# Head of a hybrid decoder layer: first weight unit in fp32, two chunks by turns, x blocks in pairs

## The chip, the cores and the metric

The kernel runs on one core of a Trainium2 chip. The metric is the device time of one execution in microseconds (us). The five engines of the core have in-order instruction queues of their own: PE multiplies matrices (PEld is its weight load), DVE and ACT do element-wise work, POOL fills memory here, and SP issues nearly all transfers (DMAs).

## The reference

One layer of a decoder trunk, for a sequence of 256 rows and a width of 1024, in fp32:

```
proj = x @ w_in                 # 1024 -> 5120, split into q k v z_a u z_s g_a g_s
y_a  = (attention(q, k, v) * silu(z_a)) @ w_attn_proj
y_s  = s5_ssm(u, ...)           # a state space scan over the rows
y_s  = glu(gelu(y_s) @ w_glu)
y_s  = (y_s * silu(z_s)) @ w_ssm_proj
mix  = (sigmoid(g_a) * y_a + sigmoid(g_s) * y_s) @ w_out
ple  = sigmoid(x @ w_ple_gate) * (p @ w_ple_proj)
out  = layer_norm(alpha * x + mix + ple)
```

What matters here is the first product, `x @ w_in`, and of it the columns of u (512) and of z_a (512). The kernel calls z_a `za`. All products have to keep nearly fp32 precision.

## The kernel before, in words

**Products by split operands.** To multiply in a fast reduced-precision type, fp32r, each operand is split: ACT rounds it to fp32r (the high half: `xh`, `whi`), and DVE subtracts that from the original (the low half: `xl`, `wlo`). A product is then three passes: high by high, low x by high weight, high x by low weight. A few small products, such as those with the tile `Kbd`, are taken in plain fp32.

**Weight units and steps.** The weights are cut into units of 256 rows by 512 columns (512 KB, in the tile `raw`, with 5 buffers). `load_next` issues the load of the next unit on SP, and `split_next` splits it on ACT (line 144) and DVE (line 145) into `whi` and `wlo` (3 buffers each). Each unit has one step on PE: two blocks of 128 rows (k), for each three passes, and for each pass four column blocks, so 24 matmuls (line 149 is the helper that issues every matmul). Four steps make a chunk of 512 columns of `w_in`. The order of the chunks is u, za, zs, q, k, v and so on. In the first chunks (`t_chunk`) x is the moving operand, 256 columns wide, and the weight is the stationary one. A chunk adds up in two PSUM banks of the kind `acc` (4 in all; 4 more, `aux`, are for other work), and when its last step is done, an evacuation (`ev_u`, `ev_za`, ...) brings it to SBUF.

**The head.** Sixteen warm-up matmuls on constants come first (line 87). x is loaded transposed in 8 blocks of 128 KB into `xs` (the tag `sc`). For c = 0 to 3 the code loads, for each of the two k, one block of x and one half of weight unit c, by turns (lines 189 and 191; the very first half in two pieces), and splits the x block (lines 192 and 193). Units 0 and 1 are split in the head in pieces. That is 18 loads; the parameters `par` (line 197) come among them, and unit 4 follows.

**The loop.** For each step i it loads the next unit, evacuates the chunk that ended, and splits a unit that is two steps ahead; then it issues the matmuls of step i, and then other work that is put to a step by number (`at(i, ...)`): parameter loads and scalar work of the state space part after step 0, `s5_bounce` (u is written to DRAM and read back in another order by eight loads, line 449) after step 4, and so on. PE runs in the order of the code. The order on the other engines, SP's queue among them, is laid out by a planner that simulates the schedule at build time, with priorities; head and loop duties have a high one.

Of the kernel before, what the change touches and what calls it, by code (L numbers as in the profile page):

```python
# [10 lines left out]
F32 = mybir.dt.float32  # L11
# [3 lines left out]
AF = mybir.ActivationFunctionType  # L15
# [3 lines left out]
P = 128  # L19
# [38 lines left out]
def hybrid_layer_kernel(ctx: ExitStack, tc, xT, x, pT, w_in, w_ap, w_sp, w_out, par, bp, cp,  # L58
                        dsk, w_glu, w_pg, w_pp, lng, lnb, relb, cst, out):
    nc = tc.nc  # L60
    V, A, G, PE = nc.vector, nc.scalar, nc.gpsimd, nc.tensor
# [5 lines left out]
    def T(shape, tag, dt=F32, bufs=1, nm=None):  # L67
        cnt[0] += 1
        return pool.tile(list(shape), dt, name=f"{nm or tag}_{cnt[0]}", tag=tag, bufs=bufs)

    def PS(tag, bufs):
        cnt[0] += 1
        return ps.tile([P, 512], F32, name=f"{tag}_{cnt[0]}", tag=tag, bufs=bufs)

    def acc():
        return PS("acc", 4)
# [19 lines left out]
    NRAW, NHI, NLO = 5, 3, 3  # L96
    units = []

    def add_units(w, k, c0, n):
        v = w.rearrange("(k p) n -> p k n", p=P)  # L100
        for k0 in range(0, k // P, 2):
            units.append(v[:, k0:k0 + 2, c0:c0 + n])
# [3 lines left out]
    raw, hi, lo = {}, {}, {}  # L106
    st = dict(load=0, split=0)

    def load_next(pieces=1):
        i = st["load"]  # L110
        if i >= len(units):
            return
        st["load"] += 1
        t = T([P, 2, 512], "raw", bufs=NRAW)
        for k in range(pieces):
            w = 2 // pieces
            nc.sync.dma_start(t[:, k * w:k * w + w], units[i][:, k * w:k * w + w])
        raw[i] = t
# [3 lines left out]
    def split_next(pieces=1):  # L122
        i = st["split"]
        if i >= len(units):
            return
        st["split"] += 1
        r = raw.pop(i)
        j = i - (len(units) - 4)
        if j < 0:
            h = T([P, 2, 512], "whi", F32R, NHI)  # L130
            l = T([P, 2, 512], "wlo", F32R, NLO)
        else:
            if j == 0:
                tail_w.update(h0=T([P, 2, 2, 512], "xh", F32R), h1=T([P, 2, 2, 512], "xl", F32R),
                              l0=T([P, 2, 2, 512], "tb", F32R), l1=T([P, 2, 2, 512], "sc", F32R))
            h, l = tail_w[f"h{j // 2}"][:, j % 2], tail_w[f"l{j // 2}"][:, j % 2]
        if pieces == 1:
            cuts = [(slice(0, 2), slice(0, 512))]
        else:
            cuts = [(slice(0, 1), slice(0, 512)), (slice(1, 2), slice(0, 512))]  # L140
            if i == 0:
                cuts[0:1] = [(slice(0, 1), slice(0, 256)), (slice(0, 1), slice(256, 512))]
        for k, c in cuts:
            A.activation(h[:, k, c], r[:, k, c], AF.Copy)  # L144
            V.tensor_sub(l[:, k, c], r[:, k, c], h[:, k, c].bitcast(F32))  # L145
        hi[i], lo[i] = h, l

    def mm(o, a, b, start, stop):
        return PE.matmul(o, a, b, start=start, stop=stop, skip_group_check=True)  # L149


    add_units(w_in, D, COL["u"], 512)
    add_units(w_in, D, COL["za"], 512)
    add_units(w_in, D, COL["zs"], 512)
    add_units(w_in, D, COL["q"], 512)
    add_units(w_in, D, COL["k"], 512)
# [23 lines left out]
    xh = T([P, KD, S], "xh", F32R)  # L180
    xl = T([P, KD, S], "xl", F32R)
    xs = T([P, KD, S], "sc")
    pr = T([P, 3, GP], "par")
    for c in range(4):
        t = T([P, 2, 512], "raw", bufs=NRAW)
        raw[c] = t
        for k in range(2):
            kk = 2 * c + k
            nc.sync.dma_start(xs[:, kk], xT[:, kk])  # L189
            for cc in ((slice(0, 256), slice(256, 512)) if kk == 0 else (slice(0, 512),)):  # L190
                nc.sync.dma_start(t[:, k, cc], units[c][:, k, cc])  # L191
            A.activation(xh[:, kk], xs[:, kk], AF.Copy)  # L192
            V.tensor_sub(xl[:, kk], xs[:, kk], xh[:, kk].bitcast(F32))  # L193
        if c < 2:
            split_next(2)
        if c == 1:
            nc.sync.dma_start(pr, par)
    st["load"] = 4
    load_next()
    br = T([P, 2, GP, 16], "brw")  # L200
    cr = T([P, 2, GP, 16], "crw")

# [160 lines left out]
    def s5_bt(part):  # L363
        b = st5["b"]
        o = st5[f"Bt{part}"] = T([P, 8, 2, 4, 16], f"A{part}")
        t = T([P, 2, 8, 4, 16], f"B{part}")
        for r in range(2):
            g = slice(8 * r, 8 * r + 8)
            ar = bc(st5["Ar"][:, g, 0:4], 3, 16)
            ai = bc(st5["Ai"][:, g, 0:4], 3, 16)  # L370
            b0, b1 = bc(b[:, part, g], 2, 4), bc(b[:, 1 - part, g], 2, 4)
            V.tensor_mul(o[:, :, r], b0, ar)
            V.tensor_mul(t[:, r], b1, ai)
            (V.tensor_add if part else V.tensor_sub)(o[:, :, r], o[:, :, r], t[:, r])
# [247 lines left out]

    steps = []

    def t_chunk(nk, xop, evac):
        st_ = {}

        def step(i, k0, first, last):
            def f(u):
                if first:  # L630
                    st_["a"] = [acc(), acc()]
                xh_, xl_ = xop()
                for k in range(2):
                    kk = k0 + k
                    for a_, b_, z in ((hi[u], xh_, 0), (hi[u], xl_, 1), (lo[u], xh_, 2)):
                        for m in range(4):
                            o = st_["a"][m // 2][:, 256 * (m % 2):256 * (m % 2) + 256]
                            mm(o, a_[:, k, m * P:(m + 1) * P], b_[:, kk, :],
                               first and k == 0 and z == 0 and m % 2 == 0,
                               last and k == 1 and z == 2)  # L640
            return f
        for i in range(nk // 2):
            steps.append([step(i, 2 * i, i == 0, i == nk // 2 - 1), None])
        steps[-1][1] = lambda: evac(st_["a"])
# [24 lines left out]
    xop = lambda: (xh, xl)  # L669
# [59 lines left out]
    def new(key, tag, shape=(P, 2, 512), dt=F32):  # L729
# [3 lines left out]
        return f  # L733

    t_chunk(8, xop, ev_u)
    t_chunk(8, xop, ev_za)
    t_chunk(8, xop, ev_zs)
    t_chunk(8, xop, ev_q)
    t_chunk(8, xop, ev_k)
# [89 lines left out]
    def at(i, *f):  # L829
        order.setdefault(i, []).extend(f)  # L830
# [8 lines left out]
    at(0, *[hp_(f) for f in (s5_scalars, s5_angles, s5_phases)])  # L839
    at(1, hp_(s5_abar))  # L840
    at(2, lambda: s5_bt(0), lambda: s5_bt(1))
    at(4, s5_bounce)
    at(8, a_bias)
    at(5, lambda: s5_ca(0), lambda: s5_ca(1))
    at(6, small_loads)
# [22 lines left out]
    for i, (f, ev) in enumerate(steps):  # L868
        with tc.high_priority():
            load_next()  # L870
            if pend is not None:
                pend()
                pend = None
            split_next(2 if i < 2 else 1)
        f(i)
        for fn in order.pop(i, []):
            fn()
        pend = ev
# [62 lines left out]
    u = nmain  # L941
# [70 lines left out]
```

## Time and profile before

| | before |
|---|---|
| median of 3 runs | 241.86 us (241.4 to 242.76) |
| the profiled execution, its own time | 242.09 us |
| its span, first to last instruction | 240.3 us |
| PE busy | 230.3 us (96%) |
| DVE busy | 188.2 us (78%) |
| ACT busy | 140.2 us (58%) |
| read from HBM | 42.47 MB, 183 GB/s over the span |

The span is what the trace covers; 1.8 us of the execution's time lie around it. Times in the rows below count from the start of the span. A matmul's duration includes the way through the array, so several overlap, and the pace is read from their starts.

### The profile page before, as it was taken

To read this page: it belongs to the slowest core of one execution; us is meant where nothing else is said; L and a number is where in the kernel's file an instruction comes from. 1 tells how busy PE (TensorE), PEld (TensorE's weight loads), DVE (VectorE), ACT (ScalarE), POOL (GpSimd) and SP (SyncE) were. 2 spreads that over 40 slices of the span, in tenths; PEclk is the share of its full clock that TensorE was granted. 3 is DMA by queue.
4 is the path that set the end of the run, shared out by engine and by line. 5 is a ranking of instruction groups with operands and counts; after the bars stand their busy time and mean duration, and the time that the engine had idled before them with its cause. 6 is when DMAs were issued, how large, how long until landed. Compare 5 with 4: busy or idle time off the path is not lost.

```text
span 240.3 us, 5066 instructions
## 1 busy us (share of the span) xinstructions
PE 230.3 (96%) x2042; PEld 212.6 (88%) x2042; DVE 188.2 (78%) x333; ACT 140.2 (58%) x222; POOL 15.9 (7%) x17
## 2 busy tenths in 40 slices
PE   8899999999999999999999999999999999999970
PEld 6899999999978899998998999999888889988760
DVE  2879999999899986878999744485674479997395
ACT  4847554845588389999734955335565353775021
POOL 4000000000000005000000000072000000000031
PEclk9999999999999999999999999999999999999998
DMA  5999998977634484323743663664555655660013
GB/s 162 331 343 357 354 238 242 353 232 215 196 93 118 147 255 119 110 92 97 232 150 136 207 213 110 197 245 162 189 174 191 199 202 170 186 190 0 3 44 131
DMA packets 26374, 44.37 MB, mean 185 GB/s; under 512 B 4200, under 2 KB 7280, under 8 KB 26352
## 3 DMA queue, kind: packets, MB, share of 16 engines
q1 hardware_dynamic: 26064, 43.75, 57.5%
q8 instruction: 16, 0.26, 0.4%
q10 hardware_dynamic: 288, 0.31, 0.4%
q14 instruction: 6, 0.05, 0.1%
HBM read 42.47 MB, written 1.59 MB: 183 GB/s over the span
## 4 chain that ended last, share of the span: by engine, by line
PE 77%; ACT 10%; DMA 5%; DVE 4%; SPq 2%; issue 1%; ACTq 0%
PE acc L149 68%; PE aux L149 8%; DMA raw<-in_w_in 5%; ACT whi L144 4%; ACT sc L587 2%; ACT sc L592 2%; ACT CAb L436 1%; DVE wlo L145 1%; SPq L191 1%; SPq L189 1%; DVE xb L930 1%; DVE xb L920 1%; DVE st L910 1%; DVE xb L908 1%; PE aux L598 0%
## 5 line engine op out<-in xcount | busy, mean ns | idle before, releaser
L144 ACT ACTIVATE whi<-raw 128x1024 fp32r<-128x1024 f32 (+2 forms) x71 | 70.7, 997 | 59.9 <-PE acc L149 52.9
L145 DVE TENSOR_TENSOR wlo<-raw,whi 128x1024 fp32r<-128x1024 f32 (+2 forms) x71 | 81.9, 1154 | 30.3 <-ACT whi L144 29.9
L149 PE MATMUL acc<-xh,whi 128*128 128x256 f32 x288 | 47.7, 287 | 0.8 <-ACT whi L144 0.8
L149 PE MATMUL acc<-xl,whi 128*128 128x256 f32 x288 | 45.8, 281 | 0.0
L149 PE MATMUL acc<-xh,wlo 128*128 128x256 f32 x288 | 45.6, 280 | 0.0
L149 PEld LDWEIGHTS acc<-xh,whi 128*128 128x128 f32 x288 | 39.3, 190 | 2.3 <-ACT whi L144 1.3
L149 PEld LDWEIGHTS acc<-xl,whi 128*128 128x128 f32 x288 | 39.3, 189 | 0.0
L149 PEld LDWEIGHTS acc<-xh,wlo 128*128 128x128 f32 x288 | 38.9, 188 | 0.3 <-DVE wlo L145 0.3
L149 PE MATMUL acc<-whi,xh 128*128 128x512 f32 x48 | 19.0, 395 | 0.0
L149 PE MATMUL acc<-wlo,xh 128*128 128x512 f32 x48 | 19.0, 395 | 0.0
L149 PE MATMUL acc<-whi,xl 128*128 128x512 f32 x48 | 19.0, 395 | 0.0
L149 PEld LDWEIGHTS acc<-wlo,xh 128*128 128x128 f32 x48 | 9.0, 188 | 2.2
L149 PEld LDWEIGHTS acc<-whi,xh 128*128 128x128 f32 x48 | 9.0, 188 | 2.1
L149 PEld LDWEIGHTS acc<-whi,xl 128*128 128x128 f32 x48 | 9.0, 188 | 2.1
L149 PE MATMUL acc<-whi,BT 128*128 128x512 f32 (+1 forms) x32 | 9.1, 366 | 0.0
L818 POOL TENSOR_SCALAR xb<-xb 128x1024 f32<-128x1024 f32 x2 | 5.5, 2774 | 42.2 <-DMA xb<-in_x 42.2
L916 ACT ACTIVATE rs<-mv,eps 128x1 f32<-128x1 f32 x2 | 0.6, 294 | 12.1 <-DVE mv L915 12.1
L587 ACT ACTIVATE sc<-sc,nmx 128x128 f32<-128x128 f32 (+1 forms) x16 | 7.0, 442 | 0.0
L149 PEld LDWEIGHTS acc<-whi,BT 128*128 128x128 f32 x32 | 5.7, 188 | 1.1
L193 DVE TENSOR_TENSOR xl<-sc,xh 128x256 fp32r<-128x256 f32 x8 | 3.4, 420 | 4.1 <-ACT xh L192 4.1
L908 DVE TENSOR_TENSOR xb<-acc,xb 128x512 f32<-128x512 f32 (+1 forms) x4 | 2.5, 619 | 5.0 <-PE acc L149 5.0
L928 POOL TENSOR_TENSOR xb<-xb,lng 128x512 f32<-128x512 f32 (+1 forms) x2 | 1.7, 839 | 69.8 <-ACT xb L927 69.8
(254 smaller groups left out, 407.8 us busy)
## 6 DMA issues: line engine op xcount, KB each, us to landing
raw<-in_w_in SPq DMA_DIRECT2D x36, 512.0 KB, 4.7
raw<-in_w_pg SPq DMA_DIRECT2D x8, 512.0 KB, 4.6
raw<-in_w_out SPq DMA_DIRECT2D x8, 512.0 KB, 4.5
raw<-in_w_ap SPq DMA_DIRECT2D x4, 512.0 KB, 5.0
raw<-in_w_glu SPq DMA_DIRECT2D x4, 512.0 KB, 3.9
raw<-in_w_sp SPq DMA_DIRECT2D x4, 512.0 KB, 4.1
raw<-in_w_in SPq DMA_DIRECT2D x7, 256.0 KB, 4.3
sc<-in_xT SPq DMA_DIRECT2D x8, 128.0 KB, 4.0
```

The costliest lines, as they stand in the source:

```text
L144: A.activation(h[:, k, c], r[:, k, c], AF.Copy)
L145: V.tensor_sub(l[:, k, c], r[:, k, c], h[:, k, c].bitcast(F32))
L149: return PE.matmul(o, a, b, start=start, stop=stop, skip_group_check=True)
L189: nc.sync.dma_start(xs[:, kk], xT[:, kk])
L191: nc.sync.dma_start(t[:, k, cc], units[c][:, k, cc])
L193: V.tensor_sub(xl[:, kk], xs[:, kk], xh[:, kk].bitcast(F32))
L436: A.activation(o[rw, :, :, 16 * g2:16 * g2 + 16], st5[f"CA{part}"][rw, :, 1:5, :], AF.Copy)
L587: A.activation(sc[:, h, qs[q]], sc[:, h, qs[q]], AF.Exp, bias=nmx[:, h, q:q + 1], accum_out=sm_[:, h, q:q + 1])
L592: A.activation(sc[:, h, qs[q]], sc[:, h, qs[q]], AF.Copy, scale=sm_[:, h, q:q + 1])
L818: G.tensor_scalar(late["xb"][:, s, :], late["xb"][:, s, :], ALPHA, None, op0=ALU.mult)
L908: V.tensor_tensor(out=xb[:, s, sl], in0=(yo2 if c0 else yo[s][n])[:, 0:c1 - c0], in1=xb[:, s, sl], op=ALU.add)
L910: V.bn_stats(out=stat[s][:, c // 256, :], in_=xb[:, s, c:c + 256])
```

## The change

The first weight unit is no longer split: it stays in fp32 in `w0`, and step 0 multiplies it by the unsplit x, `xs`, in one fp32 product in place of three passes. The units and the steps of the chunks u and za are put by turns (u, za, u, za, ...), so that two steps in a row read the same two blocks of x; za adds up in `aux` banks. x blocks 2 to 7 are loaded in pairs, and units 1, 2 and 3 as one transfer each. The x splits of blocks 4 to 7 are done in steps 2 and 4. `s5_bounce` comes after step 8.

```
@@ units @@
 add_units(w_in, D, COL["u"], 512)
 add_units(w_in, D, COL["za"], 512)
+units[:] = [units[i + 4 * c] for i in range(4) for c in range(2)]
@@ head @@
-for c in range(4):
-    t = T([P, 2, 512], "raw", bufs=NRAW)
-    raw[c] = t
-    for k in range(2):
-        kk = 2 * c + k
-        nc.sync.dma_start(xs[:, kk], xT[:, kk])
-        for cc in ((slice(0, 256), slice(256, 512)) if kk == 0 else (slice(0, 512),)):
-            nc.sync.dma_start(t[:, k, cc], units[c][:, k, cc])
-        A.activation(xh[:, kk], xs[:, kk], AF.Copy)
-        V.tensor_sub(xl[:, kk], xs[:, kk], xh[:, kk].bitcast(F32))
-    if c < 2:
-        split_next(2)
-    if c == 1:
-        nc.sync.dma_start(pr, par)
-st["load"] = 4
+def load_xT(k0, n=1):
+    nc.sync.dma_start(xs[:, k0:k0 + n], xT[:, k0:k0 + n])
+def split_x(k):
+    A.activation(xh[:, k], xs[:, k], AF.Copy)
+    V.tensor_sub(xl[:, k], xs[:, k], xh[:, k].bitcast(F32))
+w0 = T([P, 2, 512], "raw", bufs=NRAW)
+for k in range(2):
+    load_xT(k)
+    nc.sync.dma_start(w0[:, k], units[0][:, k])
+st.update(load=1, split=1)
 load_next()
+load_xT(2, 2)
+nc.sync.dma_start(pr, par)
+load_next()
+load_next()
+load_xT(4, 2)
+load_next()
+load_xT(6, 2)
+for k in (0, 1):
+    split_x(k)
+split_next(2)
+for k in (2, 3):
+    split_x(k)
@@ t_chunk @@
-def t_chunk(nk, xop, evac):
+def t_chunk(nk, xop, evac, bank=acc):
-                    st_["a"] = [acc(), acc()]
+                    st_["a"] = [bank(), bank()]
-                for a_, b_, z in ((hi[u], xh_, 0), (hi[u], xl_, 1), (lo[u], xh_, 2)):
+                for a_, b_, z in (((hi[u], xh_, 0), (hi[u], xl_, 1), (lo[u], xh_, 2)) if u
+                                  else ((w0, xs, 0),)):
@@ chunks and order @@
-t_chunk(8, xop, ev_za)
+t_chunk(8, xop, ev_za, aux)
+steps[:] = [steps[i + 4 * c] for i in range(4) for c in range(2)]
-at(4, s5_bounce)
+at(8, s5_bounce)
@@ loop @@
-        split_next(2 if i < 2 else 1)
+        if i in (2, 4):
+            for k in (i + 2, i + 3):
+                split_x(k)
+        split_next()
```

## Rows read from the trace of the kernel before

**Rows 1.** The page: busy time, share of the span and instructions.

```profile
PE 230.3 (96%) x2042; PEld 212.6 (88%) x2042; DVE 188.2 (78%) x333; ACT 140.2 (58%) x222; POOL 15.9 (7%) x17
```

**Rows 2.** Chain of waits in order of time: start, us, what.

```profile
9.83 6.41 DMA raw<-in_w_in
...
18.72 13.46 PE acc L149 x112
```

**Rows 3.** Waits, 18.72 to 228 us: us in total, times, longest.

```profile
ACT whi L144 <- PE acc L149: 52.9, 35, 3.2
```

**Rows 4.** Timeline of PE in the head: start, us, instructions, idle before.

```profile
7.39 0.74 PE L149 MATMUL acc<-xh,whi 128*128 128x256 f32 x4 [0.81 <-ACT whi L144]
...
8.91 0.63 PE L149 MATMUL acc<-xh,whi 128*128 128x256 f32 x4
...
11.73 0.63 PE L149 MATMUL acc<-xh,whi 128*128 128x256 f32 x4
...
17.46 0.74 PE L149 MATMUL acc<-xh,whi 128*128 128x256 f32 x4
...
18.72 0.74 PE L149 MATMUL acc<-xh,wlo 128*128 128x256 f32 x4
```

**Rows 5.** Timeline of PE, narrow windows at a plain fp32 product.

```profile
135.46 0.59 PE L149 MATMUL aux<-uT,Kbd 128*128 128x256 f32 x2
...
135.67 0.70 PE L149 MATMUL aux<-uT,Kbd 128*128 128x256 f32 x3
...
135.89 0.71 PE L149 MATMUL aux<-uT,Kbd 128*128 128x192 f32 x4
```

**Rows 6.** Timeline of PE, narrow windows in step 0.

```profile
5.17 0.81 PE L149 MATMUL acc<-xl,whi 128*128 128x256 f32 x3
...
5.38 0.72 PE L149 MATMUL acc<-xl,whi 128*128 128x256 f32 x3
...
5.94 0.63 PE L149 MATMUL acc<-xh,wlo 128*128 128x256 f32 x4
```

**Rows 7.** Timeline of SP: its twelfth and thirteenth load, and unit 6.

```profile
5.88 0.43 SPq L191 DMA_DIRECT2D raw<-in_w_in  x1
...
6.70 0.33 SPq L189 DMA_DIRECT2D sc<-in_xT  x1
...
10.87 0.41 SPq L117 DMA_DIRECT2D raw<-in_w_in  x1
```

**Rows 8.** Timeline of ACT and DVE in the head: splits, idle before.

```profile
5.88 0.42 ACT L192 ACTIVATE xh<-sc 128x256 fp32r<-128x256 f32 x1 [1.35 <-DMA sc<-in_xT]
...
6.70 0.63 ACT L144 ACTIVATE whi<-raw 128x512 fp32r<-128x512 f32 x1 [0.41 <-DMA raw<-in_w_in]
...
16.35 1.06 ACT L144 ACTIVATE whi<-raw 128x1024 fp32r<-128x1024 f32 x1 [2.02 <-DMA raw<-in_w_in]
...
17.44 1.22 DVE L145 TENSOR_TENSOR wlo<-raw,whi 128x1024 fp32r<-128x1024 f32 x1 [1.29 <-ACT whi L144]
```

**Rows 9.** Windows: busy of PE, PEld, DVE, ACT, POOL, clock, DMA share, GB/s.

```profile
0.00:4.00 4.00, 3.24 (x16) 2.27 (x16) 0.46 (x5) 1.96 (x3) 2.88 (x6) 1.00 0.42 121
4.00:6.70 2.70, 2.57 (x14) 2.27 (x12) 1.33 (x4) 0.88 (x3) 0.00 (x0) 1.00 0.81 238
6.70:10.14 3.44, 2.75 (x23) 2.75 (x24) 2.73 (x9) 2.81 (x7) 0.00 (x0) 1.00 1.04 350
10.14:16.25 6.11, 6.11 (x54) 6.11 (x54) 5.61 (x23) 3.36 (x7) 0.00 (x0) 1.00 0.95 323
16.25:20.30 4.05, 4.00 (x33) 3.67 (x32) 2.56 (x5) 3.21 (x6) 0.00 (x0) 1.00 1.05 396
```

**Rows 10.** DMA issues of units 4 and 6: KB each, us to landing.

```profile
raw<-in_w_in SPq DMA_DIRECT2D x1, 512.0 KB, 6.4
...
raw<-in_w_in SPq DMA_DIRECT2D x1, 512.0 KB, 9.4
```

**Rows 11.** Instructions at tile U: durations in ns, first and last start.

```profile
L149 PE MATMUL aux<-U,BT x128: 217/218/267, 93.2 to 105.8; 64*64 64x64 f32 x128
```

## The prediction

> **What bounds the kernel now.** I read the page first: the tensor engine is counted busy for 230.3 of 240.3 us [rows 1]. Such a share alone says little, so the chain of waits in order of time comes next [rows 2]. Before 18.72 its longest piece is a weight load of 6.41 us, and the split of that load ends last. At 18.72 a run of 112 matmuls begins, and the chain stays on PE for most of what follows. The waits after 18.72 agree: ACT waits 52.9 us, in 35 places, for matmuls to free weight buffers before it splits the next unit [rows 3]. So everything from 18.72 on follows the tensor engine's own pace, and the changed stage is worth what it moves that start.
>
> The timeline gives the pace. A step (one weight unit, 24 matmuls of 256 columns) takes 11.73 - 8.91 = 2.82 us, 0.1175 us for each matmul [rows 4]. In the head, step 0 stops half way and goes on at 7.39, after 0.81 us of idle time. Step 1 starts at 8.91. Step 4 starts at 17.46, but its ninth matmul, the first that needs the low half, starts only at 18.72; at the pace it would come 8 x 0.1175 = 0.94 us after the first [rows 4]. So the stream of before is worth an unbroken start of step 4 at 18.72 - 0.94 = **17.78**. The task is to find that moment after the change. It has two clocks: the matmuls and the loads.
>
> **Part 1: unit 0 without a split.** Removed: three ACT pieces, three DVE pieces and 24 matmuls. Added: 8 products in full fp32. The trace has the same kind, the Kbd products of the scan's output: each stands there as two instructions, which for 256 columns start 0.215 us apart (135.67 after 135.46, then 135.89) [rows 5]. Eight products are 16 instructions, 16 x 0.215 = 3.44 us against 2.82 us, so the edit costs PE 0.62 us. From below, two passes at the 0.1175 us of a split matmul would be 1.88 us; I take the row, which has the same tile and the same number of columns. The Trainium skill (FP8 and Floating Point Precision, TensorE Precision Notes) says true fp32 takes four passes through the array. Four passes of 0.1175 us for eight products would be 3.76 us, 0.32 us more than the row gives; the two instructions of the trace, each at nearly double time, agree in kind, and the row decides.
>
> The granted clock reads 1.00 throughout [rows 9], but early matmuls start 0.21 us apart (5.17, then 5.38) and from 5.94 on at the pace of the later steps [rows 6]: 1.2 GHz first, 2.4 GHz from about 5.81, after the engine had worked without a break from 0.8 us on. The first four matmuls therefore began at 5.17 - 4 x 0.215 = 4.31, right behind the warm-up matmuls, and an earlier operand can't move that. Fp32 instructions at the low clock should need 0.43 us (double the row): (5.81 - 4.31) / 0.43 = 3.5 of the first block's eight; the other 4.5 take 0.97 us, so the block ends at 6.78. The second block needs the second x block and weight piece, and takes 8 x 0.215 = 1.72 us: step 0 ends at **8.50**. That is 0.41 us before the 8.91 of before, although the sum of its work grew, since no split stands between load and matmul. Steps 2, 3 and 4 could then start at 11.32, 14.14 and 16.96 (2.82 apart), if their operands are there: 17.78 - 16.96 = 0.82 us gained at most.
>
> **Part 2: the order and size of the loads.** With the chunks by turns, steps 0 and 1 read the same two x blocks, so x blocks 2 and 3 are needed one step later. On SP the head has 12 issues where it had 19. SP shows a limit: its twelfth and thirteenth loads start at 5.88 and 6.70, the moments when the fourth (an x block) and the fifth (a weight piece) have landed, as ACT's waits there show [rows 7, 8]. Eight transfers are in flight at a time; larger ones put more bytes in flight. After the change the ninth to twelfth wait for the first to fourth, so all of 3.7 MB can be issued by about 6.2.
>
> Now bytes. By the windows 484 kB had moved at 4.0 us (4 x 121), 1127 kB at 6.7, and the rate is 350 GB/s from there to 10.14 [rows 9]. The fifth load landed at 6.70 and it and all before it are 786 kB, so a load lands when 341 kB more than its own end have moved. That lag grows with the bytes in flight: the load issued at 9.83 landed 6.4 us later, at 16.25, when 4305 kB had moved and 3694 were needed (611); the one issued at 10.87 landed 9.4 us later, at 20.3, with 5909 moved for 4742 (1167) [rows 7, 9, 10]. For after I take 484 kB at 4.0, 300 GB/s to 6.7 (between the 238 of before, when SP had less in flight, and 350), and 350 from there: 1294 kB at 6.7.
>
> The ends in the new order: second weight piece 786, unit 1 1311, x blocks 2 and 3 1573, parameters 1598, unit 2 2122, unit 3 2646, x 4 and 5 2908, unit 4 3432, x 6 and 7 3695, unit 5 4219 kB. The second weight piece lands at 6.14 (lag 341), before 6.78: no gap in step 0. Unit 1 lands at 6.7 + (1652 - 1294) / 350 = 7.72; its first half is split on ACT in 0.63 us [rows 8], ready at 8.40, just ahead of 8.50. Unit 2 is the tight one: it is now split whole, 1.06 us on ACT and then 1.22 us on DVE [rows 8], so its low half is ready 2.33 us after landing with the hand-overs, and step 2 wants it at 11.32 + 0.94 = 12.26: the landing must not be after **9.93**. With a lag of 341 to 611 it lands between 10.04 and 10.81; I take 10.4. Step 2 then stands still for about 0.45 us. Unit 3 lands at 12.3 with a lag of 611 and has until 14.14 + 0.45 + 0.94 - 2.33 = 13.2; unit 4 (14.6) has until 16.0. Unit 5 is new in one point: its buffer is freed by the last fp32 matmul at 8.50, not by a split, and nothing of the head stands behind it on SP. It needs 4830 kB and lands at 16.8 (18.4 with a lag of 1167), wanted by 19.78 + 0.45 + 0.94 - 2.33 = 18.84.
>
> **Part 3: what is only moved.** The x splits of blocks 4 to 7 (0.42 us a block on ACT [rows 8], and as much on DVE if its time for the same tile is like ACT's) move into steps 2 and 4, two steps ahead of their use, where ACT waits for PE; without that cover each pair would cost about 1.7 us. The u evacuation and the nine transfers of the bounce move four steps, about 11 us, later; the first matmul that reads their result starts at 93.2 [rows 11], so this is hidden, and the parameter loads keep their place behind step 0. The za chunk takes two aux banks instead of acc banks at a time when one aux bank at most is wanted elsewhere. These come to nothing.
>
> **Sum.** 0.82 gained less 0.45 for unit 2: 0.37 us. The profiled execution took 242.09 us with a span of 240.3, so its counterpart is a span of 239.9 and 241.7 us; the median shown is 241.86, which gives 241.5.
>
> **The rivals.** (a) The loads are ample: SP's larger transfers run at 350 GB/s from 4.0 on with a lag of 341, unit 2 lands at 9.65, no stall: 241.0. For it speaks that 350 is reached where the queue is full; against it the slow stretch 4.0 to 6.7. (b) Ample loads, and step 0 shorter too: with the higher clock by 5.0 it ends at 8.07, and the gain is 1.25: 240.6. Nothing in the rows moves the clock forward; cheaper fp32 instructions would do the same, against [rows 5]. (c) The other side: more bytes in flight hold the early ones back. With the lag of 1167 kB already at unit 2, it lands at 6.7 + (3289 - 1294) / 350 = 12.4, step 2 waits 2.5 us, and the kernel is 1.65 us slower: 243.5. It decides from a landing of 10.75 (no gain) and counts as slower from 11.96. Against it: lags that large came only after several transfers of 512 KB. (d) The fp32 passes keep the low clock: 16 x 0.43 from 4.31 ends at 11.19, step 4 starts at 19.65, 1.87 us later: 243.7. The rows show fp32 products only inside a stream already at the higher clock; against it, PE has no gap before them. (e) The change does nothing because the planner orders ACT and DVE anew and a later step pays back the gain: about 241.9.
>
> **How the numbers follow.** Forecast 0.43, with its own range 241.1 to 241.9; (a) 0.16; (b) 0.16; (c) 0.12; (d) 0.06; (e) 0.07. 0.5% is 1.21 us, about what a measurement here can tell from no change; faster ends at 240.65 and slower begins at 243.07. (b) is faster with 0.16 and a little of (a) and of the lower end of the forecast adds 0.02: 0.18. (c) and (d) are slower: 0.18. The rest, 0.64, is the same. The range 240.5 to 243.1 leaves out (c) and (d) and little else.
>
> **What would show it.** Right: two fp32 instructions per product 0.215 us apart, step 0 ending near 8.5, a single short stop before the low half of unit 2, then an unbroken stream to beyond 70 us, about 0.4 us ahead. Wrong: a stop between the two blocks of step 0, unit 2 landing after 10.75, 0.43 us spacing beyond 6 us, or a wait of PE after 25 us that was not there.

## The result

The changed kernel takes 243.53 us in the median (242.49 to 244.07) where the kernel before takes 241.86, seven executions of each: the ratio is 1.0061, 95% interval 1.0034 to 1.0087. Measured once more, beside the last experiments, it was 243.85 us and 1.0070 (1.0051 to 1.0089). The prediction was 241.5 us, a gain too small to count as a change; the change makes the kernel 1.7 us slower. Two executions of it have a trace: 244.01 us with a span of 242.2, and 243.32 us with a span of 241.5. Ratios leave out executions more than 1.5% above the fastest of their kernel; here these are two of the first try at theory L, the one with its trace among them.

The page's shares say nothing of it, as they answer to [rows 1] within 1.5%:

```profile
PE 230.8 (95%) x2034; PEld 211.7 (87%) x2034; DVE 186.8 (77%) x328; ACT 138.3 (57%) x217; POOL 15.9 (7%) x17
```

Where the time went is read from two places in the chain of waits (start, us, what). The kernels before and after both have there, unbroken, a run of 312 matmuls that takes 42.49 us, and far behind it one of 372 matmuls that takes 61.37 us. They cut a span into a head, a middle and a tail. First the chain of the kernel before, further on than [rows 2]:

```profile
32.70 42.49 PE acc L149 x312
...
156.78 61.37 PE acc L149 x372
```

Then that of the changed kernel, with its head:

```profile
4.02 7.79 DMA raw<-in_w_in
11.81 0.02 issue
11.83 1.07 ACT whi L144
12.90 0.02 issue
12.92 1.24 DVE wlo L145
14.16 0.04 issue
14.20 2.15 PE acc L149 x16
...
33.84 42.49 PE acc L149 x312
...
158.76 61.37 PE acc L149 x372
```

The head ends at 33.84 us in place of 32.70. The middle, from one run to the other, takes 158.76 - 33.84 = 124.92 us in place of 124.08. The tail (242.2 - 158.76 = 83.4, 240.3 - 156.78 = 83.5) is the same. So of the 1.9 us between these two traces the head has 1.14 and the middle 0.84. The second trace of the changed kernel has its run of 312 at 32.95 and a middle of 125.09; a second kernel with the head of before (the experiment with p late, below) has 32.88 and 123.92. In the means the head costs 0.6 us (33.40 against 32.79) and the middle 1.0 (125.0 against 124.0): 1.6 of the 1.7 us.

**The head after**, the timeline of TensorE (TensorE, ScalarE and VectorE are the engines that the rows call PE, ACT and DVE). The rows answer to [rows 4]:

```profile
4.59 0.67 PE L149 MATMUL acc<-sc,raw 128*128 128x256 f32 x2 [0.32 <-DMA raw<-in_w_in]
...
4.88 0.59 PE L149 MATMUL acc<-sc,raw 128*128 128x256 f32 x2
...
5.09 0.60 PE L149 MATMUL acc<-sc,raw 128*128 128x256 f32 x2
...
6.93 0.67 PE L149 MATMUL acc<-sc,raw 128*128 128x256 f32 x2 [0.38 <-DMA raw<-in_w_in]
...
9.14 0.74 PE L149 MATMUL aux<-xh,whi 128*128 128x256 f32 x4 [0.24 <-ACT whi L144]
```

Each fp32 product is indeed two instructions, 0.21 us apart. Step 0 ends near 6.93 + 8 x 0.215 = 8.65 (8.50 was forecast). Step 1 starts only at 9.14, since it waits for the split of unit 1, which ScalarE begins at 8.46 (a landing at 7.72 was forecast). Then the chain above: unit 2, issued at 4.02, lands at 11.81, its splits follow at once, and the first matmul that needs its low half starts at 14.20. From there on the engine does not stop before the middle. The loss of the head in this trace follows from this one landing: without it step 4 could have started at 9.14 + 3 x 2.82 = 17.60, still 0.18 us ahead of the 17.78 of before. How much had moved by then is in the windows (busy time of PE, PEld, DVE, ACT and POOL, granted clock, DMA share, GB/s), which answer to [rows 9]:

```profile
0.00:4.00 4.00, 3.24 (x16) 2.25 (x16) 0.23 (x4) 1.57 (x2) 2.88 (x6) 1.00 0.44 122
4.00:6.90 2.90, 2.23 (x10) 1.44 (x8) 0.85 (x2) 0.55 (x2) 0.00 (x0) 1.00 0.89 301
6.90:8.44 1.54, 1.51 (x7) 1.39 (x8) 0.00 (x0) 0.00 (x0) 0.00 (x0) 1.00 0.90 271
8.44:10.00 1.56, 1.32 (x10) 0.91 (x9) 0.69 (x1) 1.15 (x2) 0.00 (x0) 1.00 0.98 358
10.00:11.81 1.81, 1.81 (x17) 1.81 (x17) 1.28 (x7) 0.72 (x2) 0.00 (x0) 1.00 1.06 409
```

Time by rate, 488 + 873 + 417 + 558 + 740, is 3076 kB at 11.81. The forecast's own curve gives 1294 + 350 x 5.11 = 3082 there, so the rate was right. But unit 2 and all before it are 2122 kB: it landed with 954 kB of later loads already moved.

**The middle after.** TensorE's timeline has one long stop, and ScalarE's shows what came late. The longest stop of TensorE in this stretch of the trace of before is 0.47 us, at 80.28; near this one it has 0.23 us, at 112.77.

```profile
111.83 0.72 PE L149 MATMUL acc<-xh,whi 128*128 128x256 f32 x4 [1.04 <-ACT whi L144]
```

```profile
85.82 1.07 ACT L396 ACTIVATE BT<-aux 128x512 f32<-128x512 f32 x2
88.11 0.63 ACT L227 ACTIVATE ph<-Ct 128x512 fp32r<-128x512 f32 x1 [1.23 <-DMA Ct<-in_pT]
88.76 1.28 ACT L598 ACT_TABLE_LOAD   x1
90.06 0.40 ACT L598 ACTIVATE sc<-sc,nmx 128x128 f32<-128x128 f32 x1
...
110.73 2.94 ACT L144 ACTIVATE whi<-raw 128x1024 fp32r<-128x1024 f32 x3
```

The split of p (`ph`) stands in ScalarE's queue ahead of the table load and the exponentials of the softmax, and waits 1.23 us for p's transfer. From 88.11 to the split at 110.73 that TensorE waits for, ScalarE has no idle time, so the wait is passed on in full. The load itself is late because p is put into the tile `Ct`, which the state space part uses too: it is issued at 84.16, when VectorE's last reading of that tile (82.9 plus 1.22 us) has ended (the rows of the tile, and SP's timeline). In the trace of before the two moments lie as close, 85.47 behind 84.2 plus 1.22.

```profile
L417 DVE TENSOR_TENSOR C<-C,Ct x1: 1218/1218/1218, 82.9 to 82.9; 128x1024 f32<-128x1024 f32 x1
```

```profile
84.16 0.66 SPq L226 DMA_DIRECT2D Ct<-in_pT  x1
```

In the kernel before, the planner had put the same split behind the first exponentials:

```profile
84.86 1.06 ACT L385 ACTIVATE BT<-aux 128x512 f32<-128x512 f32 x2
85.94 1.28 ACT L587 ACT_TABLE_LOAD   x1
...
89.81 0.63 ACT L216 ACTIVATE ph<-Ct 128x512 fp32r<-128x512 f32 x1 [0.72 <-DMA Ct<-in_pT]
```

So there are two theories to test. L, for the head: more bytes in flight behind unit 2 hold it back. Q, for the middle: p ahead of the softmax is what the later stop pays for.

### The profile page after: what moved, and what is told of

It reads as the page before. It is cut to its first block, busy times and chain, and to the rows that moved or that the text cites. A ratio compares the mean times of both kernels' runs of the same rounds, so it can differ in the third digit from the quotient of the medians.

```text
span 242.2 us, 5025 instructions
## 1 busy us (share of the span) xinstructions
PE 230.8 (95%) x2034; PEld 211.7 (87%) x2034; DVE 186.8 (77%) x328; ACT 138.3 (57%) x217; POOL 15.9 (7%) x17
## 4 chain that ended last, share of the span: by engine, by line
PE 77%; ACT 10%; DVE 5%; DMA 5%; SPq 1%; issue 1%; ACTq 0%
PE acc L149 66%; PE aux L149 10%; DMA raw<-in_w_in 3%; ACT sc L598 3%; ACT whi L144 2%; ACT CAb L447 2%; ACT sc L603 2%; DMA Ct<-in_pT 2%; DVE wlo L145 1%; DVE xb L946 1%; DVE xb L936 1%; DVE st L926 1%; DVE xb L924 1%; ACT L598 1%; SPq L186 1%
## 5 line engine op out<-in xcount | busy, mean ns | idle before, releaser
L145 DVE TENSOR_TENSOR wlo<-raw,whi 128x1024 fp32r<-128x1024 f32 (+1 forms) x66 | 80.2, 1216 | 32.0 <-ACT whi L144 32.0
L144 ACT ACTIVATE whi<-raw 128x1024 fp32r<-128x1024 f32 (+1 forms) x66 | 68.6, 1045 | 63.1 <-PE acc L149 50.7
L149 PE MATMUL acc<-xh,whi 128*128 128x256 f32 x248 | 40.6, 285 | 1.7 <-ACT whi L144 1.7
L149 PE MATMUL acc<-xh,wlo 128*128 128x256 f32 x248 | 39.4, 280 | 0.1
L149 PE MATMUL acc<-xl,whi 128*128 128x256 f32 x248 | 39.2, 280 | 0.0
L149 PEld LDWEIGHTS acc<-xh,whi 128*128 128x128 f32 x248 | 33.4, 188 | 3.1 <-ACT whi L144 2.2
L149 PEld LDWEIGHTS acc<-xh,wlo 128*128 128x128 f32 x248 | 33.5, 188 | 0.5 <-DVE wlo L145 0.5
L149 PEld LDWEIGHTS acc<-xl,whi 128*128 128x128 f32 x248 | 33.5, 188 | 0.0
L603 ACT ACTIVATE sc<-sc,sms 128x128 f32<-128x128 f32 (+1 forms) x16 | 6.1, 442 | 0.0
```

What stands on the lines that cost most here:

```text
L603: A.activation(sc[:, h, qs[q]], sc[:, h, qs[q]], AF.Copy, scale=sm_[:, h, q:q + 1])
```

## The experiments

In the tables of times "run of 312" is the start of that run in the profiled execution, or of the run of 288 that begins at the same step; "middle" is from there to the run of 372. Ratios are to the kernel before, beside which each was measured.

**One part at a time.** Unit 0 in fp32 alone, in the head of the kernel before:

```
+if c == 0:
+    raw0.append(raw.pop(0)); st["split"] = 1      # unit 0 isn't split
...
+                    else ((raw0[0], xs, 0),)):      # step 0: one product
```

> The kernel before with only unit 0 taken in fp32 without a split; order and size of the loads stay. If the price of the fp32 passes is what costs (16 x 0.215 = 3.44 us against 2.82): 242.5. If step 0 hides it, because its halves wait for loads anyway and no split stands between: step 1 starts at 8.5 to 8.9 and the time is 241.5 to 241.9.

The two chunks by turns alone (units and steps by turns, za in `aux`, `s5_bounce` after step 8):

> The kernel before with only the chunks u and za by turns, za in aux banks, and the bounce after step 8; loads keep their sizes and units 0 and 1 their splits. Theory L: the head is as before or up to 0.3 us earlier, since nothing more is in flight: 241.6 to 241.9. Theory P (the order of work itself, through the planner, costs the later 0.8 us at 104 to 113 us): 242.7, with ACT's split in front of step 31 queued behind normalisations of the attention.

The loads alone (x blocks 2 to 7 in pairs, units 1 to 3 whole, unit 0 in two parts; three passes, chunks one after the other):

```
+nc.sync.dma_start(xs[:, kk:kk + 2], xT[:, kk:kk + 2])
+nc.sync.dma_start(t, units[c])
```

> The kernel before with only the sizes of the head's loads changed: x blocks 2 to 7 in pairs, units 1 to 3 as one transfer each, unit 0 as two; steps and splits in the old order. Theory L: unit 1 lands near 8.9 (it needs 1573 kB, with a lag of some 500), steps 1 and 2 stop, the head is 0.8 to 1.5 us later: 242.7 to 243.4. Rival B: unit 1 lands as its second half did, at 9.0, but its first half was ready 1.1 us sooner before, so 0.5 us at most: 242.4.

| | median us | ratio, interval | run of 312 | middle |
|---|---|---|---|---|
| fp32 alone | 245.48 | 1.0132 (1.0109 to 1.0155) | 32.22 | 129.22 |
| turns alone | 241.87 | 0.9987 (0.9971 to 1.0002) | 32.17 | 124.46 |
| loads alone | 246.76 | 1.0176 (1.0150 to 1.0202) | 32.96 | 127.96 |

None of the three alone costs the head more than 0.2 us against the mean of 32.79, and in these traces two of the parts cost the middle 4 to 5 us that the whole change does not (in the medians 3.3 and 4.6 us, against 242.20 beside them; the trace of fp32 alone is of its longest execution, 246.75). The waits of TensorE behind 60 us (engine, line, waited for: us in total, times, longest) say where, here for fp32 alone:

```profile
PE aux L149 <- ACT ks L720: 2.4, 1, 2.4
PE aux L387 <- DVE nmx L581: 1.3, 1, 1.3
PE aux L387 <- ACT BT L389: 1.1, 1, 1.1
```

All of it is work between 77 and 89 us (`ks` and `nmx` are tiles of the attention, `BT` one of the state space part) whose instructions no edit touched. Behind the stops its granted clock reads 0.66 from 90 to 95 us, so a part of the loss is the lower of its two levels. In the two kernels that lose, VectorE and ScalarE have another order there, though the code of that stretch is the same; with the turns alone it is nearly that of before.

**Theory L, first try: units 1 to 4 in two loads of 256 KB each, x blocks singly.**

```
-load_next(); load_xT(2, 2)
+load_next(2); load_xT(2); load_xT(3)
...
```

> The changed kernel with the same order of loads, but units 1 to 4 in two transfers of 256 KB each and x blocks one by one, so that the limit of eight transfers holds fewer bytes in flight. Theory L (bytes in flight: a load lands late when many bytes behind it are already issued; unit 2 landed at 11.8 us with 3076 kB moved where 2122 were needed): unit 2 lands by 10.8, the stop before step 2 shrinks from 0.68 + 0.25 us to 0.3 or less, the head is about 1.0 us earlier, 242.5 us if the later loss of 0.8 us stays, 241.7 if it goes. Rival B (only order and rate count): unit 2 lands at 11.8 again, 243.5.

Measured: 248.63 to 255.25 us, ratio 1.0321 (1.0270 to 1.0372). The trace is of an execution of 254.98 us; whether the shorter ones stop as long is not shown. ScalarE's timeline shows both halves of the answer:

```profile
10.35 1.06 ACT L144 ACTIVATE whi<-raw 128x1024 fp32r<-128x1024 f32 x1 [0.96 <-DMA raw<-in_w_in]
...
19.77 2.00 ACT L144 ACTIVATE whi<-raw 128x1024 fp32r<-128x1024 f32 x2 [5.96 <-DMA raw<-in_w_in]
```

Unit 2 is there at 10.33, 1.5 us earlier, as L says. But the second half of unit 4, issued at 10.48, landed at 19.6. More loads in the queue are one reason that it was issued late. The other is the planner's order: SP issues two loads of 512 KB, units 5 and 6, at 9.54 and 10.02, between the halves of unit 4 (9.1 us from issue to landing, 6.5 and 7.4 for those two). TensorE stopped for 3.18 us, and behind the stop the granted clock fell to the lower level for some microseconds (windows of TensorE and the others; the seventh value is the clock):

```profile
20.00:24.00 4.00, 3.12 (x14) 3.12 (x15) 3.14 (x8) 3.44 (x6) 0.00 (x0) 0.50 0.76 246
24.00:28.00 4.00, 4.00 (x27) 4.00 (x26) 4.00 (x9) 1.68 (x3) 0.00 (x0) 0.68 0.78 256
```

**Theory L, second try: nothing in flight behind unit 2.** Each load behind it waits for a one-element copy: x blocks 4 to 7 and units 3 and 4 for one that needs unit 1's split, the parameters of the state space part for one that needs unit 2's.

```
+def hold(dst):
+    V.tensor_copy(dst, hi[1][:, 0, 0:1].bitcast(F32))
...
+hold(t[:, 0, 0:1]); nc.sync.dma_start(t, units[i])
```

> The changed kernel with the loads behind unit 2 (unit 3, x blocks 4 to 7, unit 4, parameters of the scan) held back until unit 1 or unit 2 has landed and been split, by a copy of one element into their buffers; sizes and all else as in the changed kernel. Only the head is read, since the planner orders the middle anew. Theory L: with at most 2122 kB issued until then, unit 2 lands by 10.3 us in place of 11.8, step 2 follows step 1 without a stop, and the run of 312 matmuls, which starts at 33.84 in the changed kernel and at 32.70 before, starts by 33.0. Rival B (order and rate alone set the landing): unit 2 lands at 11.8 again and that run starts at 33.8 or later.

One execution: 252.75 us. The windows up to unit 2's landing (DMA issues of it: 512 KB, 6.2 us after 4.02):

```profile
0.00:4.00 4.00, 3.24 (x16) 2.20 (x16) 0.45 (x5) 1.70 (x2) 2.88 (x6) 1.00 0.46 129
4.00:6.00 2.00, 1.59 (x8) 1.17 (x7) 0.46 (x2) 0.42 (x1) 0.00 (x0) 1.00 0.80 193
6.00:8.44 2.44, 2.21 (x11) 1.66 (x10) 0.17 (x1) 0.34 (x1) 0.00 (x0) 1.00 1.03 383
8.44:10.18 1.74, 1.74 (x14) 1.45 (x13) 1.41 (x9) 1.43 (x4) 0.00 (x0) 1.00 0.49 166
```

516 + 386 + 935 + 289 = 2126 kB at the landing, where 2122 were needed: with next to nothing behind it, the lag is gone. The landing at 10.2 is no earlier than in the first try, because the queue runs dry (166 GB/s at the end). The held loads then paid: unit 4 was issued at 11.49, landed at 21.2, TensorE stopped for 4.62 us, and the clock was at 0.50 behind it (24 to 28 us). Here too the planner had put units 5 and 6 ahead of unit 4, as SP's timeline shows (line 214 is the held load, line 117 the loop's):

```profile
10.54 0.90 SPq L117 DMA_DIRECT2D raw<-in_w_in  x2
11.49 0.47 SPq L214 DMA_DIRECT2D raw<-in_w_in  x1
```

Both tries moved unit 2 as L says, in one trace each, and lost more at unit 4. How much of that loss is due to the smaller or held loads and how much to the two units ahead of it was not separated.

**Theory P for the middle: too much ScalarE work ahead of that split.** The four normalisations of the last pair of heads, which stand ahead of it in the changed kernel, go behind it:

```
+with tc.issue_after(last[0].ins):   # the split of unit 32
+    a_norm(hp)
```

> The changed kernel with one edit of the order on ACT: the four normalisations of the last head pair (two heads, two pieces each; 1.6 us) are queued behind the split of unit 32 and not ahead of it. Theory P (0.8 us of the loss comes from this order): PE's stop of 1.04 + 0.25 us at 111 us goes or falls below 0.3, and the time is 242.3 to 242.8. Rival (the middle only repeats the delay of the head): 243.5, and the stop shows up in front of the next step.

Measured: 245.26 us, ratio 1.0147 (1.0129 to 1.0165), run of 312 at 33.64, middle 125.82. The stop at 111 us is gone: counted from the run of 312, the first matmul there comes 1.4 us earlier than in the changed kernel. But the softmax results come later and TensorE waits for them twice (`pt`, 0.31 and 0.60 us) soon after; the middle is 0.9 us longer, not shorter. So the order is one reason for that stop, but P falls as a cure: ScalarE is late as a whole, and a change of its order at the end only moves the stop.

**Theory Q: p late.** The load and both splits of p, wanted by no product before step 36, move from step 6 to 36.

```
-at(6, small_loads)                  # with p's load; its splits followed
+at(6, small_loads); at(36, p_loads)
```

In the kernel before:

> The kernel before with the load and the split of p moved from step 6 to step 36, out of the stretch in which ACT has no idle time (90 to 113 us). If ACT sets the pace there, its 0.72 us of waiting and 0.63 us of splitting come off the stop of PE at 112.8, which is only 0.23 us: at most 0.3 us, 241.6 to 241.9. If the wait holds back more than that: 241.2.

In the kernel before with the chunks by turns:

> Chunks by turns alone, as in the run before, and the load of p moved to step 36. The head of the turns alone was 0.5 us ahead at 60 us and gave it back by 113 us, where PE waits for ACT. If p is what eats it: 241.1 to 241.4. If the order of the attention's work on ACT does: 241.9 again.

In the changed kernel:

> The changed kernel, with the load of p and its two splits moved from step 6 to step 36, so that ScalarE no longer waits for that transfer (88.11 us in the changed kernel's trace, after 1.23 us of waiting) ahead of the softmax. Theory Q (the wait for p holds up ScalarE's softmax chain, which then has no idle time until the weight split that TensorE waits for at 111.83 us): the table load of the softmax comes at about 86.9 us in place of 88.76, TensorE's 1.04 us of waiting there and the 0.3 us behind it go, and the time falls by about 0.8 us to 242.7. Rival P (ScalarE simply has too much work ahead of that split, whenever it begins, and its order is what differs): the stop stays within 0.3 us of 1.04, and the time stays at 243.5. The head should be the same in both: the run of 312 products starts at 33.8 us.

With unit 0 in fp32 alone:

> The kernel before, with unit 0 in fp32 alone and p late. With unit 0 in fp32 alone the head ended 0.48 us earlier and the middle lost some 5 us, in stops of TensorE for ks (2.42 us), nmx (1.32) and BT (1.06), the last two behind the transfer of p in the chain of waits. Theory Q (the transfer of p is a good part of it): the last two go, and the time falls from 245.5 to about 243.1. Rival P (the new order of work on VectorE and ScalarE is the cause, and p only stands in it): no change beyond 0.5 us, 245.0 to 246.0.

| p late in | median us | ratio, interval | run of 312 | middle |
|---|---|---|---|---|
| before | 241.72 | 0.9997 (0.9986 to 1.0008) | 32.88 | 123.92 |
| turns alone | 241.71 | 0.9980 (0.9962 to 0.9999) | 32.87 | 123.82 |
| the changed kernel | 241.69 | 0.9991 (0.9968 to 1.0014) | 33.23 | 123.05 |
| fp32 alone | 244.94 | 1.0134 (1.0119 to 1.0149) | 32.78 | 126.79 |

In the changed kernel the edit is worth 1.9 us (the middle 123.05 against 124.92 and 125.09). That is what p took on ScalarE ahead of that split, 1.23 us of waiting and 0.63 us of work, and not the wait alone. The idle time of 1.04 us understates it: the first matmul of that step starts at 109.68 in place of 111.83, the first with the low half at 110.71 in place of 113.09, 1.5 and 1.8 us earlier than the head accounts for. The twelve executions spread from 240.33 to 243.62 us. ScalarE's timeline:

```profile
85.20 1.07 ACT L398 ACTIVATE BT<-aux 128x512 f32<-128x512 f32 x2
86.29 1.28 ACT L600 ACT_TABLE_LOAD   x1
...
108.25 2.95 ACT L144 ACTIVATE whi<-raw 128x1024 fp32r<-128x1024 f32 x3
```

The table load follows the `BT` copies at once, and the split that was late at 110.73 comes at 108.25, a gain of 2.48 us of which 0.61 is the earlier head of this execution; 1.87 is left. Of TensorE's waits behind 60 us only 0.6 us for `BT` are left. In the kernel before, where p's split never stood ahead of the softmax, the same edit does nothing. Q holds for the changed kernel. It also shows what the new order gives back: with the normalisations ahead of the split, the `pt` products, for which the kernel before waits at 112.77, come at 112.62, counted from the run of 312 at 79.39 in place of 80.07. For fp32 alone Q is not borne out: in the trace the stops for `nmx` and `BT` are gone and the 2.4 us for `ks` stay, but the ratio did not move (1.0132 and 1.0134).

**All but the loads.** Unit 0 in fp32 and the turns, loads as before, p late:

> All of the change but its loads: unit 0 in fp32 and the two chunks by turns, with the loads in the sizes of the kernel before, and p late. If the larger loads alone cost the head (theory L: more bytes in flight hold back the landing of the unit that is needed first), the head gains what the two parts gave alone, 0.48 and 0.53 us: the wait of ScalarE's split for TensorE that ended at 60.78 us in the kernel before ends at about 59.8. If the parts need each other (rival), it gains less than 0.6 us. The middle: with the order of the kernel before it would give 240.8 in all, with the loss of some 2.5 us that is left to fp32 without p by theory Q, 243.2.

Measured: 244.87 us, ratio 1.0122 (1.0107 to 1.0137), run of 312 at 32.58, middle 126.80. The two gains of the head do not add up: 0.2 us against the mean of before. They may have been scatter: with p late, which leaves the head as it is, the turns alone and fp32 alone have their run at 32.87 and 32.78. The middle has the stops for `ks` (2.4 us) and `nmx` (1.3) of fp32 alone. That leaves the order in which the planner puts the middle as their cause; this is argued and not shown, since that order was not put back by hand.

**The first loads small, the later ones large.**

> The changed kernel with only the loads that are needed first cut small again: units 1 and 2 in two parts of 256 KB each and x blocks 2 and 3 singly, units 3 and 4 and x blocks 4 to 7 as in the change; p late. Theory L (an issue waits until the load eight before it has landed, so the size of the loads sets how many bytes are in flight, and those hold back the first): unit 2 lands at about 10.4 us in place of 11.81, the step on it starts at about 11.8 in place of 12.94, no later unit is late as unit 4 was when all were cut small, and the run of 312 products starts about 1.2 us earlier than in the changed kernel, at 32.6. Rival D (what held the step was not the landing but the splits on ScalarE and VectorE behind it, or a lower clock): it starts at 33.6 or later. Rival U (a later unit comes late again): a stop of over 1 us at step 3 or 4. The time by theory L, with the middle of the changed kernel without its stop: 241.6; with the same middle: 242.4.

Measured: 245.25 us, ratio 1.0141 (1.0110 to 1.0172). None of the three theories came out clean. The trace is of its longest execution, 247.06 us, and has no run of 312, since TensorE stops again behind 30 us. In it the first weight piece itself came 0.8 us later than in the changed kernel (5.41 in place of 4.59), unit 2 landed at 11.35, and then x blocks 4 and 5, issued at 8.13, landed only at 16.16, so that step 4 was reached no earlier. As rival U has it, a later load paid; three loads of 512 KB were issued behind that one from 8.81 to 10.67. The middle was new again, with a stop of 2.3 us for `ks`.

**Fewer bytes behind unit 2, the later order kept.** Unit 2 in two loads, x blocks 4 and 5 ahead of unit 3, x blocks 6 and 7 ahead of unit 4; p late. Then the same with unit 3 in two loads as well, and the changed kernel again:

```
-load_next(); load_next(); load_xT(4, 2); load_next(); load_xT(6, 2)
+load_next(2); load_xT(4, 2); load_next(); load_xT(6, 2); load_next()
```

> The changed kernel with p late, and unit 2 in two loads of 256 KB, x blocks 4 and 5 ahead of unit 3 and x blocks 6 and 7 ahead of unit 4. Of the loads behind unit 2, unit 4 then is issued at about 8.4 us in place of 6.24, since an issue waits for the landing of the load eight before it. Theory L (bytes in flight behind a load hold it back): unit 2 lands at about 10.8 us (11.81, 11.61 and 11.19 in the three traces with the loads of the change), unit 4 still lands before its step, and the long run of 312 products starts at about 32.8 (33.84, 33.64 and 33.23); time 241.0. Rival U (what one load gains a later one pays): unit 4 lands after 16.5 us and the run starts at 33.5 or later; time 241.7 or more.

> As the kernel with unit 2 in halves, and unit 3 in halves as well. Theory L: unit 2 as there or up to 0.4 us earlier. Unit 4 is issued one load later still, at about 10 us, so rival U says most here: if it lands after 17 us, the step on it stops TensorE by 1 us or more, the run of 312 products starts at 34 or later and the time is above 242.5. If not, 241.0 as there.

> The changed kernel itself once more, beside the others: how far the landing of unit 2 (11.81 us in the first trace) and the start of the run of 312 products (33.84) differ between two executions of the same program. Two kernels with the same loads have shown 11.19 and 33.23, and 11.61 and 33.64. If the landing varies by itself, this lies between 11.1 and 12.2; if those kernels' later edits moved it, it lies within 0.1 us of 11.81. Either way TensorE stops at about 111 us for ScalarE's split, and the time is 243.5.

| | median us | ratio, interval | run of 312 | middle |
|---|---|---|---|---|
| unit 2 in halves | 240.96 | 0.9949 (0.9936 to 0.9963) | 32.70 | 123.20 |
| units 2 and 3 in halves | 240.89 | 0.9947 (0.9932 to 0.9963) | 33.56 | 123.20 |
| the changed kernel again | 243.85 | 1.0070 (1.0051 to 1.0089) | 32.95 | 125.09 |

Both beat the kernel before by 0.5%, and the changed kernel beside them by 1.2% (240.96 to 243.85). SP's queue in the first shows unit 4 issued at 8.04 in place of 6.24, when unit 1, the eighth load before it, has landed (ScalarE starts on unit 1 at 8.05); and the chain shows unit 2's second half landing at 10.67:

```profile
6.76 0.33 SPq L186 DMA_DIRECT2D sc<-in_xT  x1
8.04 0.38 SPq L117 DMA_DIRECT2D raw<-in_w_in  x1
```

```profile
4.50 6.17 DMA raw<-in_w_in
...
32.70 42.49 PE acc L149 x312
```

Unlike in the first two tries, unit 4 is ahead of units 5 and 6 here (10.12 and 10.72). In the second kernel, the landing was 11.45 in the profiled execution, no earlier than in the changed kernel, so its trace does not bear L out. But the landing did not set its head: its fp32 products ran at the low pace (last section), step 1 began at 10.08, and TensorE had no stop in the head from 4.85 on. Step 2 could not start before 10.08 + 2.82 = 12.90, 0.76 us behind the 12.14 that breaks even, and its run of 312 is 0.77 behind 32.79. Its median stands with the first kernel's.

What these two kernels show, then, is the time: with p late, 241.69 with the loads of the change, 240.96 and 240.89 with fewer bytes behind unit 2, with intervals of the ratio that do not meet and a middle that differs by 0.15 us. That the landing is what gained it is seen in one trace (10.67, outside the range of the others below) and in those of the first two tries (10.33 and 10.18); the halves, the order of the x blocks and the later issue of unit 4 were not tried one by one.

The traces with the changed kernel's loads give the scatter. The chain's row for unit 2 is 4.02 plus 7.79 in the first of the changed kernel, 6.90 in the second, 7.17 with p late, 7.59 with the normalisations behind. The kB are, as above, rate by time up to the landing, less the 2122.

| unit 2 lands at | 10.67 (halves) | 10.92 | 11.19 | 11.61 | 11.81 |
|---|---|---|---|---|---|
| kB of later loads moved by then | 487 | 545 | 665 | 789 | 954 |
| landing less the break-even of 10.75 | -0.08 | 0.17 | 0.44 | 0.86 | 1.06 |
| run of 312 less 32.79 | -0.09 | 0.16 | 0.44 | 0.85 | 1.05 |

## Why the prediction was wrong

- **Two steps failed, of like size: forecast and result differ by 2.0 us, about 1.0 in the head (a gain of 0.37 forecast, a loss of 0.6 measured) and 1.0 in the middle. The first: the lag of the loads, of unit 2 above all.** The text took 341 to 611 kB and a landing of 10.4. In the four traces with these loads it landed at 10.92 to 11.81, 11.38 in the mean, with lags of 545 to 954 kB. The two loads ahead were late too: the second weight piece came at 6.91 for 6.14 and unit 1 at 8.44 for 7.72, with 575 and 467 kB in place of 341. The text had read that lags grow with the bytes in flight [rows 7, 9, 10] and had the case as rival (c), at 0.12, with the remark that such lags came only after several transfers of 512 KB. Here one 512 KB unit is ahead of it and two are issued within 2.2 us behind it. The lag was taken from what is issued ahead of a load; what is issued behind it moves in the same time (4 kB with nothing behind it). What is queued behind does not fix the size of the lag by itself: the same loads gave 545 and 954 kB in two executions of one program.
- **Of the rest of the head's sum, the break-even was right and the gain of 0.82 was not.** The break-even landing of 10.75 and the rule that each microsecond beyond it is one of TensorE fit the five traces of the table within 0.02 us. The rate fits within 0.2% at 11.81 (in the second trace it is 4% lower, 2667 kB at 10.92). But step 1 came at 9.14 in the first trace and 8.60 in the second, not at 8.50, so with unit 2 in time 0.18 and 0.72 us were there to gain. Units 3, 4 and 5 stopped nothing, and the moved x splits and the moved bounce cost nothing that shows.
- **Fp32 without a split.** Two instructions per product 0.215 us apart: right. That the first block would run at half the pace until about 5.8 us: wrong in this trace, where 0.21 us holds from the second instruction on, and too short in another (last section), whose head it put 0.76 us behind the break-even: rival (d), the low clock, came there in part. In the first trace step 0 ended 0.15 us later than forecast, because its second half came late (a wait of 0.38 us at 6.93). The sign shown under "wrong", a stop between the two blocks, is this one; it cost nothing, since unit 2 was later still.
- **The second step that failed: "then an unbroken stream".** The sum has nothing for the middle; it lost 0.8 to 1.0 us against before. Rival (e) named the mechanism, a planner that orders ScalarE and VectorE anew, but gave it 0.07 and let it do no more than pay back the gain. In the whole change the split of p, which waits for its load ahead of the softmax, costs 1.9 us, of which the new order gives back 0.9, most of it at the `pt` products. The waits after 18.72 in the trace of before [rows 3] show slack of ScalarE in most of the span and were read as slack everywhere; from 90 to 113 us it has none.
- **Chances.** Each loss was a rival with a small chance; that both could come, 0.6 and 1.0 us, was not summed. They do come apart: the second trace of the changed kernel has nearly nothing of the first (0.16 us) and all of the second. That the measured 243.5 is the figure of rival (c) is luck: (c) has it from a landing at 12.4 and a middle without loss.

What stays open: why the order of the middle differs so between kernels whose middle is the same code, beyond the fact that it does; why the landing of the same load differs by 0.9 us between executions; and whether p in a tile of its own, loaded early, would do as well as p late.

## What to carry to other kernels

Where loads are limited in number and not in bytes, a larger load early in a queue can be paid for by the load ahead of it: cut the ones that a step waits for, keep the later ones behind them, and check each later deadline and the order in which the queue issues, since the first two cures here only moved the stop to unit 4, which two later units had overtaken. Where a planner lays out the in-order queues, an edit in one place can move a wait to the front of a busy engine somewhere else: look for an instruction that waits for a transfer at the head of a stretch without idle time, ask what holds that transfer up (here a shared tile), and give it a late place by hand. And stretches far behind the edit belong to the forecast too: here half of the miss lay some 100 us behind it.

## What the runs showed of the hardware

**Loads in flight share the rate.** The same load of 512 KB landed with 4 kB of later loads moved when none was queued behind it (one execution), and with 545 to 954 kB in four executions with 1.6 MB behind it. The Trainium skill (DMA: Bandwidth & Descriptors, Rules for kernel authors) advises to coalesce many small transfers into one large one, and names those under 64 KB. No run here shows that case: the loads of x and of the weights have 128 KB and more. Among these the traces show no difference in rate to speak of (409 GB/s at best with the loads of the change, 396 with those of before [rows 9]), and larger loads were not better for the time: with one unit in halves, and two x loads ahead of a unit each, the ratio went from 0.9991 to 0.9949.

**When the clock comes up differs between executions.** The fp32 products of step 0 were 0.21 us apart from 4.88 on in the changed kernel (above). In the kernel with units 2 and 3 in halves the same instructions, behind the same warm-up matmuls and a wait of 0.52 us, were 0.42 us apart from the second on (narrow windows of TensorE's timeline):

```profile
4.85 1.19 PE L149 MATMUL acc<-sc,raw 128*128 128x256 f32 x2 [0.52 <-DMA raw<-in_w_in]
...
5.41 1.06 PE L149 MATMUL acc<-sc,raw 128*128 128x256 f32 x2
...
5.83 1.06 PE L149 MATMUL acc<-sc,raw 128*128 128x256 f32 x2
```

That is the doubling that the prediction had expected, 1.2 and 2.4 GHz by their pace; it lasted to 8.39, and step 1 came at 10.08 in place of 9.14. The wait in front is not what made it: in the changed kernel with p late one of 0.51 us stood there, and the pace was 0.21 us from the second instruction on. The granted clock reads 1.00 in both executions, as it did in [rows 9]: in the first microseconds the pace tells the clock and that column does not. Later on the column does fall: a stop of 3.18 us brought a granted clock of 0.50 behind it, one of 1.04 us did not, and of two of 2.4 us one did (0.72 from 80 to 85 us, loads alone) and one did not (1.00 there, fp32 alone).
